# Two heads' attention scores in one step, their matmuls alternating between the two halves of TensorE's rows

## The chip, the cores and the metric

The kernel runs on one core of one Trainium2 chip. The metric is the device time of one execution in microseconds (us). Five engines work side by side: TensorE (PE in the profile, its weight loads PEld), VectorE (DVE), ScalarE (ACT), GpSimd (POOL) and SyncE (SP, which issues the weight DMAs). Each executes its own instructions in the order in which the program issues them and waits on semaphores of the others.

## The reference

Two transformer blocks run one after the other on 256 tokens of width 1024, in float32. The first has an even layer (differential attention and a convolution) and an odd one (a state space model and a latent attention), each with a gated feed-forward part. The second block has two layers. Each has two attentions over the same normalized input, both with 8 query heads of dimension 64:

```python
# kind "n": 256 own tokens with a bias, and 256 context tokens
s_win = einsum(qg, kg) * SCALE + bias;  s_ctx = einsum(qg, k_ctx) * SCALE
p = softmax(concatenate([s_win, s_ctx], -1));  o = p_win @ vg + p_ctx @ v_ctx
# kind "g": grouped, 2 key heads for 8 query heads, keys of x and of the context
s = einsum('bgrqd,bgkd->bgrqk', q, k_all) * SCALE;  o = softmax(s) @ v_all
```

Their results are merged with gates, projected, and followed by a gated feed-forward part. In the first of the two layers the 256 context tokens go through the same two attentions, but over the context alone.

## The kernel before

Activations are kept transposed (features on the 128 partitions, tokens along the free axis). Every dense product is made in three matmuls of split operands (`mm3`, L369 to L371; `token_steps`, L827 to L829): a weight is split into a high and a low part by ScalarE (`uh`, L349) and VectorE (`ul`, L350), a unit of 8 x 128 weights at a time.

The work is cut into steps held in queues, and `ORDER`, a string written out by hand, says in which order the queues give their steps: `m` is the main chain, `c` the chain of the context, `d` the modulation, `a` the attentions of the second block over x and the context, `x` the gates' projections, `k` small masks. So in the attentions of the second block, runs of `a` steps stand between single `x` or `m` steps. The program is issued in that order, and no engine reorders it for us.

`attention2` (L1844) makes the attentions of the second block. An item is a kind, one of two query tiles of 128 (`qt`) and a head. With two key sources (512 keys, n = 1) an item is one head; for the context alone (256 keys, n = 2) it is the heads h0 and h0 + 2, side by side in one PSUM bank. `pipeline` gives each item three steps: `scores`, then in the next round `trans`, then `out` one round later. Within one round the order is scores(i), out(i - 2), trans(i - 1).

- `scores` takes a PSUM bank of the tag "s" and makes per key source one float32 matmul with 64 rows: head h lies on the partitions 64 (h % 2) to 64 (h % 2) + 63. The profile shows each as two weight loads and two passes (L1861). Then it calls `softmax`.
- `softmax` (L852) puts off its work: `peak` (for kind "n" over x first the bias, L1867; maximum, L875; negation, L879) runs on VectorE, then `exp` (L869) on ScalarE. Each is issued when the steps issued meanwhile have used up a planned cost, 0.6 and then 1.0.
- `trans` forces its own item's `peak` and `exp` out if they aren't issued, takes another "s" bank, transposes the four blocks of 128 probabilities on TensorE (L893), and ScalarE copies them to SBUF (`probT`, L895). VectorE makes the reciprocal of the sums (L886).
- `out` does nothing for an even head. For an odd one it makes the products with the values of that head and the one before (L1891, 16 passes) and the reciprocals' broadcast (L1894, 4 passes) in the one bank "n"; ScalarE (L1908) and VectorE (L1903) take them out.

There are three "s" banks, taken in turn. `ps` (L203) counts the softmaxes whose `exp` is not issued and issues the oldest before a tag would run out:

```python
while tag == "s" and sum(k for _, k in self.held) + n > 3:
    self.undefer(self.held[0][0])
```

The even layer of the first block (L1041 to L1053) makes its scores in another form: two matmuls on the two halves of the rows into two banks, in one step.

Of the kernel before, what the change touches and what calls it, by code (L numbers as in the profile page):

```python
# [13 lines left out]
ALU = mybir.AluOpType  # L14
# [3 lines left out]
P = 128  # L18
T = 256
# [133 lines left out]
class Kern:  # L153
# [1690 lines left out]
    def attention2(self, st, kvs, local, kinds="ng"):  # L1844


        nc = self.nc
        d = {}
        K = T * len(kvs)
        n = 512 // K  # L1850

        def scores(it):
            kind, qt, h0 = it
            ps = self.ps("s").rearrange("p (g k) -> p g k", g=n)
            for a in range(n):
                h = h0 + 2 * a
                b = slice(64 * (h % 2), 64 * (h % 2) + 64)
                q = st[kind + "q"][b, h // 2, P * qt:P * qt + P]
                for i, kv in enumerate(kvs):
                    k = kv["nk"][b, h // 2, :] if kind == "n" else kv["gk"][b, (h // 4 + h) % 2, :]  # L1860
                    nc.tensor.matmul(ps[:, a, T * i:T * i + T], lhsT=q, rhs=k, start=True, stop=True)  # L1861
            pre = None
            if kind == "n" and local:
                def pre():
                    w = st["bias"][:, 6 * h0 + 2 - 2 * qt:6 * h0 + 6 - 2 * qt, ::-1]
                    v = ps[:, 0, :T].rearrange("p (j u) -> p j u", u=64)
                    nc.vector.tensor_tensor(v, v, w, ALU.add)  # L1867
            self.softmax(ps, n, 1.0 if kind == "n" else 0.125, K, d, it, pre)

        def trans(it):  # L1870
            self.undefer((id(d), it))
            pt, sm = d[it]
            t, r = self.transpose_prob(pt.rearrange("p g k -> p (g k)"), 512), self.recip(sm)
            for a in range(n):
                d[it[0], it[1], it[2] + 2 * a] = t[:, K * a:K * a + K], r[:, a:a + 1]

        def out(it):

            kind, qt, h0 = it
            if h0 % 2 == 0:  # L1880
                return
            o = self.ps("n").rearrange("p (a g t) -> p a g t", a=2, t=P)
            nk = K // P
            for g in range(n):
                m = h0 // 2 + g
                two = [d.pop((kind, qt, 2 * m + a)) for a in range(2)]
                for i in range(nk):
                    kv, k = kvs[i // 2], i % 2
                    for a in range(2):
                        c = 64 * (2 * m + a if kind == "n" else m // 2)  # L1890
                        nc.tensor.matmul(o[64 * a:64 * a + 64, 0, g, :], lhsT=kv[kind + "v"][:, k, c:c + 64],  # L1891
                                         rhs=two[a][0][:, P * i:P * i + P], start=i == 0, stop=i == nk - 1)
                for a in range(2):
                    nc.tensor.matmul(o[64 * a:64 * a + 64, 1, g, :], lhsT=two[a][1].to_broadcast([P, 64]), rhs=self.ident,  # L1894
                                     start=True, stop=True)
            m = h0 // 2
            if m == 0:
                d[kind, qt] = self.w2("oh", [P, 4, P])
            oh = d[kind, qt]
            R = self.w1("sr")[:, :P * n].rearrange("p (g t) -> p g t", g=n)  # L1900

            def norm():
                nc.vector.tensor_tensor(oh[:, m:m + n, :], o[:, 0, :n, :], R, ALU.mult)  # L1903
                if m + n == 4:
                    self.defer(0, lambda: st["ysink"](kind, qt, d.pop((kind, qt))))

            def factor():
                nc.scalar.activation(R, o[:, 1, :n, :], AF.Copy)  # L1908
                self.defer(0, norm)

            self.defer(0, factor, key="n")

        heads = (0, 1, 4, 5) if n == 2 else range(8)
        items = [(kind, qt, h) for kind in kinds for qt in range(2) for h in heads]
        return self.pipeline(items, [(scores, 0.86, 0), (out, 0.5 * n, 2), (trans, 0.44, 1)])

    def gate_steps(self, st, l, pool=None):

# [139 lines left out]
    def second_block(self, X, C):  # L2058

        steps = []  # L2060
        rope = lambda: (X["rC"], X["rS"])
        self.queues.update(a=[], x=[], k=[])
        keys = [dict(n="c", pn="ck", pg="ck", spill=C["spill"]) for _ in range(2)]

        def tables(l):
            if l == 0:
                self.open("ck", "right")
                self.new_kv(keys[0], ("gk", "gv", "nk", "nv"))
                for k in ("gk", "gv", "nk", "nv"):
                    self.unspill(keys[0], k, keys[0][k])  # L2070
            else:
                self.open("y2")
            self.open("pg", "left" if l else "right")
            self.open("ph", "left" if l else "right")
            X.update(pn="ph", pg="pg")
            X["rC"], X["rS"] = self.table("pg", "xc"), self.table("pg", "xs")

        def room(l):
            if l == 0:
                self.close("ar")  # L2080
                self.open("y2")
            self.open("gs", "right" if l else "left")
            self.ysplit(X, "y2")

        def end_att():
            self.close("ph")
            self.open("ph")

        def end_merge(l):
            for k in ("ph", "pg", "gs", "ck", "y2"):  # L2090
                self.close(k)
            self.open("ph")

        for l in range(2):
            load, mask = self.na_bias(X, l)
            steps.append(Step(lambda l=l: tables(l), after=[] if l else [self.spilled]))
            steps += self.modulated(X, l, 0)
            p1, p2 = self.proj_steps(X, l, rope)
            steps += [load] + p1
            steps.append(Step(lambda l=l: room(l), after=self.queues["c"][-1:]))  # L2100
            free = steps[-1]
            steps += p2
            mask[0].after.append(load)
            gates = self.gate_steps(X, l, "gs")
            gates[0].after.append(free)
            att = self.attention2(X, [X, keys[l]], True, "gn") + [Step(self.undefer)]
            att[0].after.append(p1[-1])
            for x in att[:-1]:
                fn, (kind, qt, h) = x.what
                if (fn, kind, qt) == ("scores", "n", 0):  # L2110
                    x.after += [p2[-1], mask[h]] + (last[-1:] if l else [])
                if l and x is att[0]:
                    x.after.append(self.last_a)
                if (fn, kind, qt, h) == ("out", "g", 0, 7):
                    x.after.append(free)
            self.queues["a"] += att
            self.queues["x"] += gates
            self.queues["k"] += mask
            steps.append(Step(end_att, after=[att[-1], gates[-1]]))
            steps += self.merge_steps(X, l) + self.wo_steps(X, l)  # L2120
            steps.append(Step(lambda l=l: end_merge(l)))
            if l == 0:
                last = self.last_keys(C, keys[1])
                last[0].after.append(steps[-1])
                self.queues["c"] += last
            steps += self.modulated(X, l, 1) + self.ffn2(X, l)
            steps.append(Step(lambda: self.close("ph")))
        return steps
# [143 lines left out]
```

## Time and profile before

| | |
|---|---|
| median of 3 runs | 2039.46 us (2037.99 to 2041.78) |
| the profiled execution | 2035.8 us, its span 2034.0 us |
| busy: PE, PEld, DVE, ACT, POOL | 95%, 88%, 67%, 49%, 4% of the span |
| mean granted TensorE clock | 0.978 |
| chain that ended last, by engine | PE 76%, DVE 14%, ACT 4%, DMA 4%, issue 2% |
| the same by line, L1861 | 4% |

The span runs from the first to the last instruction; the execution's own time is 1.8 us longer, and the median of the runs lies 3.7 us above that. A line such as `L893 PE MATMUL pss<-consts,prob` names the source line, the engine, the operation and the tiles written and read (`psd`, `pss`, `psn` are PSUM banks of the tags d, s, n). An end in brackets such as `[0.36 <-ACT prob L869]` is the time for which the engine was idle before it, and what ended that. The recorded time of a matmul contains its passage through the array, so matmuls that follow each other overlap in the records; what a group costs is read from its start to the start of what follows.

### The profile page before, as it was taken

The page shows a single profiled execution, that of the slowest core. Times are in us where ns is not written, and L with a number is a line of the kernel's source. Part 1 is how long each engine was busy: PE and PEld are TensorE (multiplying, and loading weights), DVE is VectorE, ACT ScalarE, POOL GpSimd, SP SyncE. Part 2 cuts the span into 40 slices and gives each one's busy share as a digit, 9 for nine tenths or more (in the row PEclk, how much of TensorE's full clock was granted, in tenths as well). Part 3 has the DMA queues.
Part 4 walks back from the last instruction along what each step waited for, and adds up shares of the span by engine and source line. Part 5 has one row for each costly group of instructions (what it writes and reads, how often), then busy time and mean ns, then how long its engine had stood idle before and what let it go on. Part 6 is the DMA issues. An engine that isn't in the chain of part 4 may idle for free.

```text
span 2034.0 us, 38003 instructions
## 1 busy us (share of the span) xinstructions
PE 1927.8 (95%) x15646; PEld 1785.2 (88%) x15646; DVE 1361.2 (67%) x2655; ACT 988.7 (49%) x1680; POOL 71.9 (4%) x112
## 2 busy tenths in 40 slices
PE   8889999999989999989996999989999899979998
PEld 7678889999878999789996888889999888879998
DVE  6997668777778678666655745676655755566554
ACT  5355665444445453554443455445444455535443
POOL 0212000000000000000001100000000100000000
PEclk9999999999989999999998999999999999999999
DMA  7756636666748665766556633345555643244553
GB/s 255 247 193 207 195 110 201 202 218 220 230 133 241 205 187 141 236 200 217 194 174 188 156 101 86 122 145 173 182 175 199 159 120 89 81 149 158 179 177 109
DMA packets 383775, 353.51 MB, mean 174 GB/s; under 512 B 14705, under 2 KB 370545, under 8 KB 383089
## 3 DMA queue, kind: packets, MB, share of 16 engines
q1 hardware_dynamic: 378336, 333.77, 51.9%
q0 software_dynamic: 4688, 15.73, 3.3%
q8 instruction: 123, 2.02, 0.4%
q10 hardware_dynamic: 576, 1.57, 0.2%
q14 instruction: 52, 0.42, 0.1%
HBM read 344.36 MB, written 6.68 MB: 173 GB/s over the span
## 4 chain that ended last, share of the span: by engine, by line
PE 76%; DVE 14%; ACT 4%; DMA 4%; issue 2%; SPq 0%; ACTq 0%; DVEq 0%
PE psd L369 21%; PE psd L371 20%; PE psd L370 20%; DVE ul L350 4%; PE pss L1861 4%; ACT uh L349 3%; PE pss L893 2%; PE psn L1891 2%; DMA raw<-in_w_in 2%; DVE cy L999 1%; PE psd L1657 1%; DMA raw<-in_l_w_in 1%; DMA raw<-in_w_mod 1%; PE psd L827 1%; DVE xres L592 1%
## 5 line engine op out<-in xcount | busy, mean ns | idle before, releaser
L350 DVE TENSOR_TENSOR ul<-raw,uh 128x1024 fp32r<-128x1024 f32 (+3 forms) x556 | 657.5, 1190 | 365.3 <-ACT uh L349 363.3
L349 ACT ACTIVATE uh<-raw 128x1024 fp32r<-128x1024 f32 (+3 forms) x556 | 566.0, 1025 | 337.1 <-PE psd L370 272.3
L369 PE MATMUL psd<-xacth,uh 128*128 128x256 f32 x2192 | 633.9, 289 | 9.9 <-ACT grp L703 3.1
L371 PE MATMUL psd<-xacth,ul 128*128 128x256 f32 x2192 | 626.2, 286 | 5.1 <-DVE ul L350 5.1
L370 PE MATMUL psd<-xactl,uh 128*128 128x256 f32 x2192 | 626.2, 286 | 0.6 <-DVE xactl L599 0.5
L369 PEld LDWEIGHTS psd<-xacth,uh 128*128 128x128 f32 x2192 | 425.8, 194 | 28.2 <-issue 13.4
L371 PEld LDWEIGHTS psd<-xacth,ul 128*128 128x128 f32 x2192 | 425.9, 194 | 6.6 <-DVE ul L350 6.5
L370 PEld LDWEIGHTS psd<-xactl,uh 128*128 128x128 f32 x2192 | 426.0, 194 | 1.9 <-DVE xactl L599 1.0
L369 PE MATMUL psd<-slot,uh 128*128 128x256 f32 x896 | 256.0, 286 | 0.5 <-ACT uh L349 0.5
L371 PE MATMUL psd<-slot,ul 128*128 128x256 f32 x896 | 251.4, 281 | 2.6 <-DVE ul L350 2.6
L370 PE MATMUL psd<-slot,uh 128*128 128x256 f32 x896 | 251.0, 280 | 0.0
L371 PE MATMUL psd<-hh,ul 128*128 128x256 f32 x704 | 198.1, 281 | 0.6 <-DVE ul L350 0.3
L369 PE MATMUL psd<-hh,uh 128*128 128x256 f32 x704 | 198.0, 281 | 0.0
L370 PE MATMUL psd<-hl,uh 128*128 128x256 f32 x704 | 197.5, 280 | 0.0
L369 PEld LDWEIGHTS psd<-slot,uh 128*128 128x128 f32 x896 | 169.6, 189 | 7.4 <-issue 5.2
L371 PEld LDWEIGHTS psd<-slot,ul 128*128 128x128 f32 x896 | 169.3, 189 | 3.3 <-DVE ul L350 3.3
L370 PEld LDWEIGHTS psd<-slot,uh 128*128 128x128 f32 x896 | 169.4, 189 | 0.0
L371 PEld LDWEIGHTS psd<-hh,ul 128*128 128x128 f32 x704 | 132.0, 188 | 1.6 <-DVE ul L350 1.6
L369 PEld LDWEIGHTS psd<-hh,uh 128*128 128x128 f32 x704 | 132.5, 188 | 0.4 <-issue 0.4
L370 PEld LDWEIGHTS psd<-hl,uh 128*128 128x128 f32 x704 | 132.5, 188 | 0.0
L869 ACT ACTIVATE prob<-pss,nm 128x512 f32<-128x512 f32 (+2 forms) x124 | 70.2, 568 | 22.3 <-DVE nm L879 18.9
L875 DVE TENSOR_REDUCE mx<-pss 128x1 f32<-128x512 f32 (+1 forms) x80 | 55.2, 689 | 34.4 <-PE pss L1861 33.2
(480 smaller groups left out, 2528.4 us busy)
## 6 DMA issues: line engine op xcount, KB each, us to landing
raw<-in_w_mod SPq DMA_DIRECT2D x48, 1024.0 KB, 5.5
raw<-in_w_ffn_in SPq DMA_DIRECT2D x40, 1024.0 KB, 5.1
raw<-in_w_in SPq DMA_DIRECT2D x32, 1024.0 KB, 5.7
raw<-in_w_ffn_in SPq DMA_DIRECT2D x52, 512.0 KB, 5.2
raw<-in_w_in SPq DMA_DIRECT2D x48, 512.0 KB, 5.2
raw<-in_w_ffn_out SPq DMA_DIRECT2D x24, 1024.0 KB, 4.9
raw<-in_l_w_gate SPq DMA_DIRECT2D x20, 1024.0 KB, 5.3
raw<-in_l_w_up SPq DMA_DIRECT2D x20, 1024.0 KB, 5.3
```

Of the source, the lines that this page charges most:

```text
L349: self.nc.scalar.activation(q.h, src, AF.Copy)
L350: self.nc.vector.tensor_tensor(q.l, src, q.h.bitcast(F32), ALU.subtract)
L369: mm(ps, lhsT=wh, rhs=ah, start=start, stop=False)
L370: mm(ps, lhsT=wh, rhs=al, start=False, stop=False)
L371: mm(ps, lhsT=wl, rhs=ah, start=False, stop=stop)
L592: nc.vector.tensor_tensor(x(m), x(m), d.pop(m), ALU.add)
L827: mm(d[i][j], lhsT=ah[:, s], rhs=u.h[:, k, :], start=kk == 0, stop=False)
L869: nc.scalar.activation(pt[:, g, :], ps[:, g, :] if one else ps[g], AF.Exp, bias=nm[:, g:g + 1], scale=scale, accum_out=sm[:, g:g + 1])
L875: nc.vector.tensor_reduce(mx, ps, AX.X, ALU.max)
L893: self.nc.tensor.transpose(t[:, k * P:(k + 1) * P], w[:, k * P:(k + 1) * P], self.ident)
L1861: nc.tensor.matmul(ps[:, a, T * i:T * i + T], lhsT=q, rhs=k, start=True, stop=True)
L1891: nc.tensor.matmul(o[64 * a:64 * a + 64, 0, g, :], lhsT=kv[kind + "v"][:, k, c:c + 64], rhs=two[a][0][:, P * i:P * i + P], start=i == 0, s ...
```

## The change

The even item's `scores` step now makes the scores of its own head(s) and of the next odd ones. It takes two banks, and the matmuls alternate between the rows 0 to 63 (even head, first bank) and 64 to 127 (odd head, second bank). Both softmaxes are put off from there, the even one first. The odd item's `scores` step does nothing. The planned cost of the step in the pipeline is 0.65 for 0.86, and the masks that the first pair of kind "n" needs are required for both heads. `ORDER` is as it was, and so are `trans` and `out`.

```diff
         def scores(it):
             kind, qt, h0 = it
-            ps = self.ps("s").rearrange("p (g k) -> p g k", g=n)
+            if h0 % 2:
+                return
+            two = [self.ps("s", 2 - j).rearrange("p (g k) -> p g k", g=n) for j in range(2)]
             for a in range(n):
-                h = h0 + 2 * a
-                b = slice(64 * (h % 2), 64 * (h % 2) + 64)
-                q = st[kind + "q"][b, h // 2, P * qt:P * qt + P]
                 for i, kv in enumerate(kvs):
-                    k = kv["nk"][b, h // 2, :] if kind == "n" else kv["gk"][b, (h // 4 + h) % 2, :]
-                    nc.tensor.matmul(ps[:, a, T * i:T * i + T], lhsT=q, rhs=k, start=True, stop=True)
-            pre = None
-            if kind == "n" and local:
-                def pre():
-                    w = st["bias"][:, 6 * h0 + 2 - 2 * qt:6 * h0 + 6 - 2 * qt, ::-1]
-                    v = ps[:, 0, :T].rearrange("p (j u) -> p j u", u=64)
-                    nc.vector.tensor_tensor(v, v, w, ALU.add)
-            self.softmax(ps, n, 1.0 if kind == "n" else 0.125, K, d, it, pre)
+                    for j in range(2):
+                        h = h0 + 2 * a + j
+                        b = slice(64 * j, 64 * j + 64)
+                        q = st[kind + "q"][b, h // 2, P * qt:P * qt + P]
+                        k = kv["nk"][b, h // 2, :] if kind == "n" else kv["gk"][b, (h // 4 + h) % 2, :]
+                        nc.tensor.matmul(two[j][:, a, T * i:T * i + T], lhsT=q, rhs=k, start=True, stop=True)
+            for j, ps in enumerate(two):
+                pre = None
+                if kind == "n" and local:
+                    def pre(ps=ps, h=h0 + j):
+                        w = st["bias"][:, 6 * h + 2 - 2 * qt:6 * h + 6 - 2 * qt, ::-1]
+                        v = ps[:, 0, :T].rearrange("p (j u) -> p j u", u=64)
+                        nc.vector.tensor_tensor(v, v, w, ALU.add)
+                self.softmax(ps, n, 1.0 if kind == "n" else 0.125, K, d, (kind, qt, h0 + j), pre)
...
-        return self.pipeline(items, [(scores, 0.86, 0), (out, 0.5 * n, 2), (trans, 0.44, 1)])
+        return self.pipeline(items, [(scores, 0.65, 0), (out, 0.5 * n, 2), (trans, 0.44, 1)])
...
-                    x.after += [p2[-1], mask[h]] + (last[-1:] if l else [])
+                    x.after += [p2[-1], mask[h], mask[h | 1]] + (last[-1:] if l else [])
```

## Rows read from the trace of the kernel before

**Rows 1.** Busy time of each engine, context attentions, a slow stretch, both layers' attentions.

```profile
core 0: us, PE busy (x) PEld busy (x) DVE busy (x) ACT busy (x) POOL busy (x), PEclk, DMA share, GB/s
178.00:316.00 138.00, 132.34 (x1080) 117.85 (x1077) 98.44 (x251) 87.08 (x208) 9.40 (x16) 0.99 0.56 173
285.80:289.90 4.10, 4.10 (x29) 3.21 (x28) 3.10 (x8) 1.91 (x6) 0.00 (x0) 0.58 0.70 227
1161.00:1300.00 139.00, 138.33 (x1066) 114.36 (x1064) 72.37 (x157) 76.14 (x150) 0.07 (x1) 1.00 0.32 92
1628.00:1767.00 139.00, 138.11 (x1076) 114.31 (x1075) 70.51 (x155) 76.56 (x151) 0.00 (x0) 1.00 0.32 92
```

**Rows 2.** Chain of waits within 1161 to 1300 us: shares by line.

```profile
by line: PE pss L1861 23.6%; PE psd L369 14.4%; PE psd L370 12.6%; PE psd L371 12.6%; PE pss L893 12.3%; PE psn L1891 11.8%; PE psd L827 3.1%; PE psd L828 2.7%; PE psd L829 2.6%; PE psn L1894 2.5%; ACT probT L895 0.8%; ACT prob L869 0.6%; i
```

**Rows 3.** Timeline of TensorE at 1628 us (start, duration, what): two heads, nothing between.

```profile
1628.45 0.71 PE L1861 MATMUL pss<-xgk,xgq 64*128 64x256 f32 x4
1628.99 0.60 PE L1861 MATMUL pss<-cgk,xgq 64*128 64x256 f32 x4
1629.52 0.50 PE L827 MATMUL psd<-uh,xacth 128*128 128x512 f32 x1
```

**Rows 4.** Timeline of TensorE at 1213 us: transposes, one head's scores, products, transposes.

```profile
1212.82 0.66 PE L893 MATMUL pss<-consts,prob 128*128 128x128 f32 x4
1213.40 0.70 PE L1861 MATMUL pss<-xgk,xgq 64*128 64x256 f32 x2
...
1214.46 0.66 PE L1891 MATMUL psn<-probT,xgv 128*64 128x128 f32 x8
...
1215.71 0.66 PE L893 MATMUL pss<-consts,prob 128*128 128x128 f32 x4
```

**Rows 5.** Timeline of TensorE at 1264 us: transposes with a gate's matmuls behind them.

```profile
1263.69 0.66 PE L893 MATMUL pss<-consts,prob 128*128 128x128 f32 x4
1264.10 0.36 PE L369 MATMUL psd<-xacth,uh 128*128 128x256 f32 x1
```

**Rows 6.** Timeline of ScalarE at 1214 us: the copy of the transposes of rows 4.

```profile
1213.57 0.60 ACT L895 ACTIVATE probT<-pss 128x512 f32<-128x512 f32 x1 [0.59 <-PE pss L893]
```

**Rows 7.** Timeline at the end of the first layer's attentions: transposes, products directly behind.

```profile
1296.89 1.09 PE L893 MATMUL pss<-consts,prob 128*128 128x128 f32 x8
...
1298.72 0.30 PEld L1891 LDWEIGHTS psn<-probT,xnv 128*64 128x64 f32 x5 [0.31 <-ACT probT L895]
...
1299.96 0.39 PE L369 MATMUL psd<-xacth,uh 128*128 128x256 f32 x1
```

**Rows 8.** Groups within 1161 to 1300 us: count, busy us, mean ns, idle before.

```profile
L350 DVE TENSOR_TENSOR ul<-raw,uh 128x1024 fp32r<-128x1024 f32 x24 | 29.4, 1224 | 13.3 <-ACT uh L349 13.3
...
L349 ACT ACTIVATE uh<-raw 128x1024 fp32r<-128x1024 f32 x23 | 24.2, 1056 | 4.3 <-PE psd L370 1.7 <-ACT prob L869 1.4 <-PE psd L829 1.2
L875 DVE TENSOR_REDUCE mx<-pss 128x1 f32<-128x512 f32 x32 | 22.1, 691 | 18.4 <-PE pss L1861 17.8
L869 ACT ACTIVATE prob<-pss,nm 128x512 f32<-128x512 f32 x32 | 21.9, 684 | 2.5 <-DVE nm L879 1.9 <-DVE ri L886 0.3
...
L895 ACT ACTIVATE probT<-pss 128x512 f32<-128x512 f32 x32 | 19.0, 597 | 18.0 <-PE pss L893 18.0
...
L1867 DVE TENSOR_TENSOR pss<-pss,bias 128x256 f32<-128x256 f32 x16 | 6.9, 432 | 16.3 <-PE pss L1861 16.3
...
L879 DVE TENSOR_SCALAR nm<-mx 128x1 f32<-128x1 f32 x32 | 4.9, 154 | 1.1
```

**Rows 9.** Timeline of TensorE at 1283 us: transposes that wait for their exponentials.

```profile
1283.49 0.66 PE L893 MATMUL pss<-consts,prob 128*128 128x128 f32 x4 [0.36 <-ACT prob L869]
```

**Rows 10.** Chain of waits within 178 to 316 us: start, duration, what.

```profile
198.19 1.07 PE pss L1861 x4
...
285.88 1.49 PE pss L1861 x4
...
311.39 1.06 PE pss L1861 x4
```

## The prediction

> **What bounds the kernel now.** I read the page first: TensorE is busy for 95% of the span and makes 76% of the chain that ended last. The attentions fill three stretches, so I read the busy time there [rows 1]: TensorE 138 of 139 us in both layers over x, against 72 and 71 for VectorE and 76 and 77 for ScalarE; 132 of 138 us where the context's attentions run among other chains. The reader is to see that in the two later stretches nothing but TensorE can set the time, at the full granted clock (2.4 GHz). The chain inside the first of them puts 23.6% on L1861, the line of the change, more than on any other [rows 2]; that is 33 us of 139 for 32 scores steps. Then I read the timeline of TensorE block by block, since the change moves blocks and leaves their order.
>
> **What two heads cost together.** One head's scores take 1.06 us from their start to the start of what follows (1213.40 to 1214.46) [rows 4]. The trace of before holds one place where two heads stand directly behind each other, at the head of the second layer: eight passes start at 1628.45 and the next matmul at 1629.52, so 1.07 us for two heads [rows 3]. The four passes over own keys are listed before the four over the context's, although the program issues all of one head first: the two halves run beside each other. So a pair costs 1.07 us, and each odd step taken out leaves the time of a whole block, less 0.01.
>
> By the Trainium skill (TensorE: Matmul & The Clock Gate, Part 3, "The mechanism") matmuls start and end strictly in program order and only weight loads overtake. Rows 3 show the second head's first passes ahead of the first head's last ones, so the trace differs from that rule here, and I go by the trace; what strict order would make of the time is a rival below.
>
> **What is taken out.** Over x there are 32 odd steps, 16 a layer; one is paired already (rows 3), so 31 go. What each is worth hangs on what stands behind it. Walking through both stretches I count 16 with a gate's or a value projection's matmuls behind them (for one of them transposes), and 15 that stand between the transposes of one odd head and `out`, which needs these very transposes.
>
> The 16: transposes to scores 0.58, scores 1.06 [rows 4]; transposes straight to a gate's matmuls 0.41 [rows 5], since no change between 64 and 128 rows is left. 0.58 + 1.06 - 0.41 = 1.23 each, 19.7 us.
>
> The 15: here the odd scores are the cover for ScalarE's copy. Transposes to `out` take 1.64 us now (1212.82 to 1214.46) [rows 4]. The copy of them starts 0.75 us after they start and takes 0.60 [rows 6], so the odd head's half of `out` can start after 1.35 plus some 0.05. The stretch's end shows the case without a scores step between [rows 7]: the second of two sets of transposes starts at about 1296.89 + 0.41 = 1297.30, the products that need its copy at 1298.72, 1.42 us later, after a wait for `probT`; from there to the next block is 1.24 us, a whole `out`. So 1.64 - 1.40 = 0.24 us is left of each, 3.6 us. Bounds: if the even head's products cover the copy, the full 1.06 (12.3 us more in all); if one weight split, 1.06 us [rows 8], always stands before the copy on ScalarE, 0.82 lost on each (15.9 us less). I take the value of rows 7: ScalarE was idle for 18.0 us before the 32 copies of a stretch, waiting for the transposes in all of it [rows 8], so it was nearly always free when they came.
>
> **What moves.** The odd head's softmax is issued one round earlier, behind the even one's. VectorE then makes two in a row: 0.43 bias, 0.69 maximum, 0.15 negation [rows 8], 1.36 with the gaps for kind "n", 0.9 without bias. The even head's transposes lie later than its exponentials in every case that I worked out. The three banks taken in turn are the new wait: two rounds take four banks, so the next pair's even scores land in the bank of this pair's odd scores and wait for its exponential. Behind them on TensorE everything queues. With no filler between, the next pair comes 1.07 + 1.40 + 1.24 + 0.58 = 4.29 us after this one; the pair's last pass ends at 1.14 (1628.99 + 0.60 - 1628.45) [rows 3], so the second "n" softmax ends at 1.14 + 2 x 1.36 + 0.68 + 0.05 = 4.59, so a wait of 0.3 to 0.45; the kind without bias ends at 3.7 and waits for nothing. Five places of kind "n" have no filler: 2 us lost. Bounds: nothing, and with a low split (1.22) before them on VectorE at the nine fillerless places of both kinds, 15. A wait that goes: the transposes at 1283.49 wait 0.36 us for an exponential that will now be long made [rows 9], and so once in the other layer: 0.7 us. No DMA is added or moved; the shares of 0.32 leave room.
>
> Over x: 19.7 + 3.6 + 0.7 - 0.3 - 2.0 = 21.7 us.
>
> **The context's stretch.** Eight odd steps go. The chain there runs through six of them; rows 10 show the first, the slow one (285.88) and the last. Two, at 182 and 294 us, are not in it: VectorE's convolution and a normalization end later there, and they bring nothing. Five at 1.06 and one at 1.49 make 6.8; row changes would add up to 1, and VectorE, 71% busy here [rows 1], may take some back. All `out` steps here have fillers before them. I take 6.3, with 0 and 9 as ends.
>
> **Sum.** 21.7 + 6.3 = 28.0 us of the profiled execution's 2035.8, so 2007.8; the runs' median lies 3.7 us higher: 2011.5 us.
>
> **The rivals.**
> - *The copy is covered* (0.08). `out` begins with the even head's products while the odd copy runs, and the waits stay away: 12.3 + 2 us more, 1997. For it: ScalarE is 55% busy. Against: rows 7, where it waited.
> - *Strict order* (0.04). A matmul's second pass must start before the other half's first, so of every two passes only one is hidden: five pass times in place of four. A pass is (1.06 - 0.17) / 4 = 0.22 us, the 0.17 being the row change (0.58 less 0.41) [rows 4, 5]; for 39 pairs 8.6 us: 2020. Rows 3 speak against it. (This is the rule of the Trainium skill named above.)
> - *Softmax takes over in the fillerless runs* (0.12). There a pair leaves TensorE some 3.5 us of work, while ScalarE needs 2 x (0.68 + 0.60) and readouts, VectorE 2 x 1.36 and reciprocals, so any extra op sets the time: 15 places at 1 us, 2026. For it: the balance in those runs; against: whole stretches have 76 us of ScalarE in what will be 128. (The Trainium skill, TensorEngine Tiling, "PSUM Bottleneck", warns that packing speeds the array and not the emptying of PSUM; by rows 1 that binds in these runs at most.)
> - *Late bank, slower* (0.05). If the odd exponential is late at every pair, with a low split in front of it on VectorE (0.4 + 1.22), all 31 pairs wait 1.6 us: 50 us lost, 2059. It decides from 0.9 us a pair (28 / 31). Against: most pairs have a filler of about 3 us between.
> - *The halves don't overlap when alternated* (0.03). Two heads then cost 2.1 us as before, only row changes go, and the 15 waits of 0.82 and the banks stay: some 11 us slower, 2050. Rows 3 speak against it.
> - *Given back later* (0.06). What follows waits for weights that can't come earlier: 2036 to 2040. For it: the DMA is 56% busy in the context's stretch; against: 32% in the other two.
>
> A fall of the granted clock belongs to the waits: 285.8 to 289.9 ran at a mean of 0.58, mostly the lower level (1.2 GHz), after an idle TensorE, and the scores there took 1.49 [rows 1, 10]. My waits are below 1 us each, and around rows 9 nothing slowed.
>
> **How the numbers follow.** Forecast 0.62, its own range 2005 to 2020. Of the 0.38 left, 0.24 is faster too. The range 2000 to 2028 takes in the softmax case, the strict order and most of the covered one. A change under 0.2% (4 us) can't be told here from none. Faster 0.87, same 0.05, slower 0.08.
>
> **What would show it.** L1861: pairs of 1.07 us at 40 places, TensorE's busy time about 30 us less. A new wait of `out` for `probT` of 0.3 to 0.8 us at 15 places, and of L1861 for `prob` at about five. Both stretches over x 11 us shorter, the context's 6. Wrong would be: pairs of 1.3 or 2.1 us, waits over 1 us at most pairs, or shorter attentions with a longer rest.

## The result: 2018.97 us, and the profile after

The median fell from 2039.17 us (4 runs) to 2018.97 us (4 runs, 2015.73 to 2025.85), a ratio of 0.9904 [0.9876, 0.9931], about 20 us; forecast were 2011.5 us and 28 us. The profiled execution after took 2025.85 us (span 2023.1), 6.9 above the median of its runs, so the two traces are compared by stretches and not by their spans.

The lines behind the change moved: the scores' matmuls are L1865 now, the bias L1872, the products L1896, the reciprocals' broadcast L1899, ScalarE's copy of it L1913, VectorE's product with that copy L1908. First the busy time of each engine in the three stretches of attentions, after (start:end, length, busy time and instructions of each engine, granted clock, DMA share, GB/s), to be held against [rows 1]. A stretch over x is cut here and below from the first scores matmul to the first matmul behind the last `out`.

```profile
core 0: us, PE busy (x) PEld busy (x) DVE busy (x) ACT busy (x) POOL busy (x), PEclk, DMA share, GB/s
178.90:317.00 138.10, 128.64 (x1102) 117.60 (x1098) 98.52 (x255) 87.36 (x208) 9.41 (x16) 0.98 0.57 173
1166.60:1296.10 129.50, 124.16 (x1058) 104.55 (x1057) 69.82 (x157) 76.14 (x149) 0.05 (x1) 1.00 0.34 99
1629.70:1756.20 126.50, 122.33 (x1069) 104.55 (x1068) 68.75 (x154) 75.70 (x149) 0.00 (x0) 1.00 0.35 101
```

Cut the same way, the stretches of before are 138.0 us (to 1299.96 [rows 7]) and 137.9 us (from 1628.45 [rows 3]). So 8.5 us went in the first layer and 11.4 us in the second. That alone is 19.9 us, all of what the medians lost. The context's stretch, cut between the same two instructions (177.14 to 316.02 us before, 177.88 to 314.31 after), is 2.5 us shorter in this trace; over all runs it gave next to nothing, as shown further down. New beside [rows 1] is that TensorE no longer fills its stretches: 5.3 and 4.2 us are idle, where 0.7 and 0.9 were.

The chain of waits within 1166 to 1296 us, shares by line, answers to [rows 2]: scores fell from 23.6% to 13.3%, while VectorE's maximum (L875) and bias (L1872), which were not listed there, now carry 9.4%.

```profile
by line: PE psd L369 13.5%; PE pss L1865 13.3%; PE psd L370 12.7%; PE psd L371 12.7%; PE pss L893 10.1%; PE psn L1896 8.9%; DVE mx L875 6.4%; PE psn L1899 3.4%; PE psd L827 3.3%; DVE pss L1872 3.0%; PE psd L828 2.8%; PE psd L829 2.8%; ACT p
```

Where the idle time comes from stands in two timelines of one place without filler. TensorE (start, duration, engine, line, operation, tiles, count, and in brackets the idle time before it and what ended it):

```profile
1256.79 0.70 PE L1865 MATMUL pss<-xnk,xnq 64*128 64x256 f32 x4
1257.32 0.60 PE L1865 MATMUL pss<-cnk,xnq 64*128 64x256 f32 x4
1257.85 0.66 PE L893 MATMUL pss<-consts,prob 128*128 128x128 f32 x4
1258.44 0.43 PE L1896 MATMUL psn<-probT,xnv 128*64 128x128 f32 x2
1259.26 0.54 PE L1896 MATMUL psn<-probT,xnv 128*64 128x128 f32 x5 [0.39 <-ACT probT L895]
...
1260.68 0.43 PE L1899 MATMUL psn<-consts,ri 128*64 128x128 f32 x2 [0.33 <-DVE ri L886]
1261.04 0.66 PE L893 MATMUL pss<-consts,prob 128*128 128x128 f32 x4
```

Eight passes cost 1.06 us (1256.79 to 1257.85), the forecast price. The products start with the even head's two passes and then wait for the odd head's copy: 1.41 us after the transposes began, the 1.40 of the forecast. But `out` doesn't end there. Its broadcast stops a second time, for the reciprocals, and the block takes 2.60 us (1258.44 to 1261.04) where it took 1.25 [rows 4]. VectorE at the same place shows why:

```profile
1257.95 0.43 DVE L1872 TENSOR_TENSOR pss<-pss,bias 128x256 f32<-128x256 f32 x1 [1.01 <-PE pss L1865]
1258.42 0.69 DVE L875 TENSOR_REDUCE mx<-pss 128x1 f32<-128x512 f32 x1
1259.14 0.15 DVE L879 TENSOR_SCALAR nm<-mx 128x1 f32<-128x1 f32 x1
1259.22 0.42 DVE L1872 TENSOR_TENSOR pss<-pss,bias 128x256 f32<-128x256 f32 x1
1259.67 0.69 DVE L875 TENSOR_REDUCE mx<-pss 128x1 f32<-128x512 f32 x1
1260.40 0.15 DVE L879 TENSOR_SCALAR nm<-mx 128x1 f32<-128x1 f32 x1
1260.47 0.21 DVE L886 RECIPROCAL ri<-sm 128x1 f32<-128x1 f32 x2
```

The sum that this `out` waits for belongs to the pair before and was made before the transposes at 1257.85 could start. But `trans` issues its reciprocal (L886) behind the new pair's two biases and maxima, and VectorE keeps that order: 2.5 us of work (1257.95 to 1260.47), where one head's 1.3 stood before.

The waits of TensorE's weight loads (waiting line, what ended the wait, total us, times, longest), first those of the first layer's stretch, then of the second's:

```profile
PEld psn L1896 <- ACT probT L895: 6.6, 11, 0.9
PEld psn L1899 <- DVE ri L886: 2.6, 5, 0.6
...
PEld psn L1896 <- ACT probT L895: 4.5, 8, 0.6
PEld psn L1899 <- DVE ri L886: 1.8, 2, 1.2
```

Now the context's stretch. Its pairs want two of the three "s" banks at once. The first pair's weight loads, after:

```profile
178.88 0.29 PEld L1865 LDWEIGHTS pss<-slot 64*128 64x128 f32 x2 [0.41 <-ACT slot L1791]
180.89 0.73 PEld L1865 LDWEIGHTS pss<-slot 64*128 64x128 f32 x6 [1.71 <-ACT prob L869]
```

The odd head's bank is held by another chain's softmax; TensorE's weight loads stand still for 1.71 us (its matmuls for 1.31) in the middle of the pair. The fifth pair waits in its middle too, for a bank that another chain's VectorE step still reads:

```profile
251.70 0.73 PEld L1865 LDWEIGHTS pss<-slot,slot 64*128 64x128 f32 x6 [0.90 <-DVE xactl L391]
```

At the other end, VectorE of after at 293 us, and the second of its maxima as it stood before:

```profile
293.20 0.68 DVE L875 TENSOR_REDUCE mx<-pss 128x2 f32<-128x512 f32 x1
...
294.00 0.68 DVE L875 TENSOR_REDUCE mx<-pss 128x2 f32<-128x512 f32 x1
...
299.66 0.68 DVE L875 TENSOR_REDUCE mx<-pss 128x2 f32<-128x512 f32 x1
```

At 299.66 us, before, it stands behind the normalization (L589 to L599) that the chain runs through here; now it stands in the middle of it. TensorE's wait there, then the busy time in slices of 2 us (columns as above), three of after and two of before:

```profile
291.65 0.80 PE L893 MATMUL pss<-consts,prob 128*128 128x128 f32 x4 [1.77 <-ACT probT L895]
...
290.00:292.00 2.00, 0.34 (x3) 0.35 (x4) 2.00 (x7) 1.20 (x3) 0.00 (x0) 1.00 0.00 0
292.00:294.00 2.00, 2.00 (x12) 2.00 (x11) 1.97 (x7) 0.81 (x2) 0.00 (x0) 0.51 0.04 8
294.00:296.00 2.00, 2.00 (x13) 2.00 (x13) 1.97 (x7) 0.36 (x1) 0.05 (x1) 0.64 0.00 0
...
292.00:294.00 2.00, 0.41 (x4) 0.17 (x3) 2.00 (x8) 1.19 (x4) 0.00 (x0) 1.00 0.00 0
294.00:296.00 2.00, 2.00 (x13) 1.61 (x14) 2.00 (x5) 1.00 (x2) 0.00 (x0) 1.00 0.04 8
```

After, TensorE was idle for most of 290 to 292 us, since the transposes there waited 1.77 us for a copy (`probT`), and then ran mostly at the lower level (1.2 GHz) until about 295. Before, the slices from 290 to 302 are all granted 1.00. An earlier fall (285.8 to 289.9 us before [rows 1], 284 to 290 after) stands in both traces and costs the same 1.7 us, counted as length times the missing share of the clock.

### The profile page after: what moved, and what is told of

Read it like the earlier page. It is cut to its first block, busy times and chain, and to the rows that moved or that the text cites. A ratio compares the mean times of both kernels' runs of the same rounds, so it can differ in the third digit from the quotient of the medians.

```text
span 2023.1 us, 37981 instructions
## 1 busy us (share of the span) xinstructions
PE 1899.8 (94%) x15646; PEld 1765.9 (87%) x15646; DVE 1358.2 (67%) x2655; ACT 989.3 (49%) x1680; POOL 72.6 (4%) x112
## 4 chain that ended last, share of the span: by engine, by line
PE 55%; DVE 9%; ACT 4%; DMA 2%; issue 2%; ACTq 0%; SPq 0%; DVEq 0%
PE psd L369 15%; PE psd L371 15%; PE psd L370 15%; DVE ul L350 3%; ACT uh L349 2%; PE pss L1865 2%; DMA raw<-in_w_in 2%; PE pss L893 1%; PE psn L1896 1%; PE psd L1657 1%; DVE mx L875 1%; PE psd L827 1%; PE psd L828 1%; PE psd L829 0%; DVE pr L1979 0%
## 5 line engine op out<-in xcount | busy, mean ns | idle before, releaser
L456 DVE TENSOR_TENSOR acc<-acc,sq 128x256 f32<-128x256 f32 x116 | 49.1, 423 | 43.2 <-ACT sq L455 41.6
```

Source lines behind the costliest of these rows:

```text
L456: self.nc.vector.tensor_tensor(acc, acc, s, ALU.add)
```

## The experiments

The theory: two heads cost the time of one because the two halves of the rows work side by side; the rest follows from what stood beside the removed steps (copy, softmax, banks). Each run is timed against before on its own chip. An edit moves the lines below it, so an operation can stand under another number in a run; its tiles name it (`pss<-xnk,xnq` are scores, `pss<-consts,prob` transposes, `psn<-probT` products).

**All of the even head first, then all of the odd head.** If the gain lay in the alternation, it would go.

```diff
-            for a in range(n):
-                for i, kv in enumerate(kvs):
-                    for j in range(2):
+            for j, a in [(j, a) for j in range(2) for a in range(n)]:
+                for i, kv in enumerate(kvs):
```

> All of the even head's matmuls are issued before the odd head's, in the same step. Theory (the two halves of the rows run side by side whatever the program order): pairs stay at 1.07 us, the time stays with the changed kernel's 2019 us. Rival (matmuls keep program order, only the alternation brings the overlap): pairs of 2.1 us, 40 of them, some 40 us more, 2060 us.

2014.2 us, ratio 0.9881 [0.9849, 0.9912]; stretches 129.3 and 126.6 us, as after. TensorE:

```profile
1259.99 0.71 PE L1865 MATMUL pss<-xnk,xnq 64*128 64x256 f32 x4
1260.53 0.60 PE L1865 MATMUL pss<-cnk,xnq 64*128 64x256 f32 x4
1261.07 0.66 PE L893 MATMUL pss<-consts,prob 128*128 128x128 f32 x4
```

1.08 us for the pair. The order within a pair is worth nothing; what counts is that both heads stand together.

**The same, with one 128-row matmul of a single column between the two heads.** It needs both halves, so the heads can't overlap. Everything else (two banks, one step, softmax earlier) stays.

```diff
+                if j and not a:
+                    nc.tensor.matmul(two[1][:, 0, 0:1], lhsT=self.ident, rhs=self.ident[:, 0:1], start=True, stop=True)
```

> As e1, but a one-column matmul over all 128 rows stands between the two heads, so that they can't overlap; the place of the steps and of the softmaxes is the changed kernel's. Theory (the whole gain is the overlap): a pair costs 2.2 us or more, 1.15 to 1.4 us more at 40 places, some 50 us more than the changed kernel, about 2065 us, slower than before by 25. Rival (the gain is that softmaxes are issued earlier): it stays below 2030 us.

2066.46 us, 1.0122 [1.0094, 1.0151]; stretches 148.6 and 146.3 us, some 19.5 us longer than after in each.

```profile
1228.98 0.70 PE L1867 MATMUL pss<-xgk,xgq 64*128 64x256 f32 x2
1229.52 0.59 PE L1867 MATMUL pss<-cgk,xgq 64*128 64x256 f32 x2
1230.04 0.38 PE L1860 MATMUL pss<-consts 128*128 128x1 f32 x2
1230.35 0.70 PE L1867 MATMUL pss<-xgk,xgq 64*128 64x256 f32 x2
1230.89 0.59 PE L1867 MATMUL pss<-cgk,xgq 64*128 64x256 f32 x2
1231.41 0.66 PE L893 MATMUL pss<-consts,prob 128*128 128x128 f32 x4
```

2.43 us for the pair in place of 1.06. Of these the added matmul takes 0.31 itself (1230.04 to 1230.35), so two heads that can't overlap cost 2.12, twice one. Without the 0.31 at 40 places, 12 us, the time would be some 2054 us, still above before's 2043.97 on that chip: without the overlap the new waits make the change a loss, and the overlap alone pays for them.

**`out` one round later.** This puts another pair between an odd head's transposes and its products.

```diff
-        return self.pipeline(items, [(scores, 0.65, 0), (out, 0.5 * n, 2), (trans, 0.44, 1)])
+        return self.pipeline(items, [(scores, 0.65, 0), (out, 0.5 * n, 3), (trans, 0.44, 1)])
```

> `out` one round later (3 for 2), the rest as changed: the next pair's scores and an even head's transposes now lie between an odd head's transposes and its `out`. Theory (15 places lose 0.8 us to the copy and some 9 of them 0.5 us more to the reciprocal behind two maxima): both waits go, each layer's attentions 6 to 9 us shorter, 2004 us. Rival (in these runs the softmax chain on VectorE and ScalarE sets the time): the wait moves to L893 for `prob`, the time stays near 2019 us.

2021.77 us, 0.9908 [0.9884, 0.9931]. Over x it gains (124.9 and 124.6 us, 6.5 in all), but two sets of transposes now stand directly behind each other, and the second waits for its exponential (6.4 us at four places of the first layer); and the context's stretch, whose `out`s come later too, loses about 9 us. A mixed run: it shows that the copy wait can be covered and that the softmax is next.

**The reciprocals issued right behind the exponentials.** If the second wait is VectorE's order, it goes.

```diff
+            if early:
+                d[it] = pt, self.recip(sm)
...
-            t, r = self.transpose_prob(pt.rearrange("p g k -> p (g k)"), 512), self.recip(sm)
+            t = self.transpose_prob(pt.rearrange("p g k -> p (g k)"), 512)
```

> The reciprocal of the sums is issued right behind its exponential and not in `trans`, where it stands behind the next pair's two maxima on VectorE. Theory: the waits of L1899 for `ri` (4 us in the first layer, 3.1 in the second) go, `out` falls from 2.60 to 2.05 us at seven places, 4 to 6 us in all: 2014 us. Rival (VectorE waits for the exponential at the head of its queue, and the low splits or the bias behind it come late): 2019 us or more.

2021.06 us, 0.9904 [0.9879, 0.9928]; stretches 128.1 and 125.5 us. The wait of the broadcast is gone, and but for one (2.33 us) no `out` takes more than 2.05 us, so the cause of that wait is shown. But only 2.4 of its 4.4 us came out of the stretches, and the median shows no gain over the changed kernel. What took the place is the late bank of the forecast, at five places of kind "n", three in the first layer and two in the second. One of them, on TensorE and in its weight loads:

```profile
1271.05 0.94 PE L1867 MATMUL pss<-xnk,xnq 64*128 64x256 f32 x3
...
1272.56 0.39 PE L369 MATMUL psd<-xacth,uh 128*128 128x256 f32 x1
...
1271.51 0.18 PEld L1867 LDWEIGHTS pss<-xnk,xnq 64*128 64x128 f32 x1 [0.17 <-ACT prob L869]
```

1.51 us for a pair that costs 1.06, since the bank it wants is still read by the last pair's exponential; the other four take 1.40 to 1.52. Together that is 1.9 us.

**The fillers spread.** The gates' and value projections' steps that `ORDER` places among the attentions over x keep their sequence, but stand one at a time (two or three early on) directly before the odd `out`s, so that each copy has a cover.

```diff
-        self.run(self.merge(self.chains(), self.ORDER))
+        self.run(self.merge(self.chains(), respread(self.ORDER, plans)))
```

`respread` rewrites the order between the first and the last `a` step of each layer: in the first, two stand before the first `trans`, then 2, 2, 3, 2 and one each before the odd `out`s; in the second two, then five times 2 and one each (the last odd `out` has none).

> The changed kernel with another order: in both layers' attentions the gate and projection steps between the attention steps stand one (early two) directly before each odd head's `out`, where 15 of them had none; their own sequence is kept. Theory (what the change gives back over x is the wait of `out` for the copy, 0.8 us at 15 places, and for the reciprocal): both waits go, each stretch falls from 129.5 and 126.5 us to 119 to 122, 2006 us. Rival (softmax on VectorE and ScalarE has become the bound of these runs): the waits move to L893 and L1865, the stretches stay above 125 us, 2017 us or more.

2002.02 us, 0.9796 [0.977, 0.9822]: 118.3 and 119.2 us, 38.4 less than before in both stretches together. Its busy time:

```profile
1172.00:1290.30 118.30, 118.30 (x1058) 102.72 (x1057) 69.39 (x157) 75.51 (x148) 0.05 (x1) 1.00 0.38 107
1614.90:1734.10 119.20, 118.80 (x1070) 103.47 (x1069) 68.36 (x154) 76.20 (x149) 0.00 (x0) 1.00 0.38 107
```

TensorE is full again. One place of it (transposes, a filler from 1255.47, `out`, transposes):

```profile
1255.06 0.66 PE L910 MATMUL pss<-consts,prob 128*128 128x128 f32 x4
...
1258.51 0.66 PE L1913 MATMUL psn<-probT,xnv 128*64 128x128 f32 x8
1259.00 0.61 PE L1913 MATMUL psn<-probT,cnv 128*64 128x128 f32 x8
1259.43 0.39 PE L1916 MATMUL psn<-consts,ri 128*64 128x128 f32 x4
1259.75 0.66 PE L910 MATMUL pss<-consts,prob 128*128 128x128 f32 x4
```

`out` takes 1.24 us, without a wait in it.

**That order in the kernel before.**

```diff
-        self.run(self.merge(self.chains(), self.ORDER))
+        self.run(self.merge(self.chains(), respread(self.ORDER, plans)))
```

> The order of e5 in the kernel before, whose heads are made one by one. Theory: TensorE waited for nothing there, so the order alone brings nothing: stretches of 137 to 139 us, 2039 us. Rival (the order is a gain of its own): below 2033 us.

2038.76 us, 0.9994 [0.9977, 1.001]; 137.0 and 138.0 us. Before, the odd scores were the cover, and another order brings nothing. Only with the pairs is it worth about 17 us by the medians (18.5 in the two stretches).

**Pairs over x alone, and pairs for the context alone** (the other kind keeps the old `scores`).

```diff
+        if n == 2:
+            return self.pipeline(items, [(single, 0.86, 0), (out, 0.5 * n, 2), (trans, 0.44, 1)])
```

and the same with `n == 1`.

> Pairs only in the attentions over x; the context's heads are made one by one as before. Theory (in the context's stretch the pairs wait for their second bank, which other chains hold, and the six steps' time is given back there): the time of the changed kernel within 3 us, 2019 us, the stretch from 178 to 316 us no longer than its own by more than 2.5. Rival (the context's pairs bring the 6 us forecast): 2025 us.

> Pairs only in the context's attentions; over x one head at a time as before. Theory: 0 to 3 us less than before, 2037 us, both stretches over x at 138 us. Rival (they bring 6 us): 2033 us.

2024.82 us, 0.9912 [0.9887, 0.9937], and 2038.15 us, 0.999 [0.9968, 1.0012]. The intervals of the first and of the whole change overlap widely, and the second holds 1: over x lies the gain, and the context's pairs bring nothing that can be measured. (The 6.3 us forecast for them would be a ratio of 0.9969, just inside that interval; the profiles, below, are the stronger evidence.)

**ScalarE's copy over x made twice**, to see whether `out` waits for it.

```diff
-        self.defer(0, lambda: self.nc.scalar.activation(o[:, :keys], t[:, :keys], AF.Copy))
+        def copy():
+            for _ in range(1 + again):
+                self.nc.scalar.activation(o[:, :keys], t[:, :keys], AF.Copy)
+        self.defer(0, copy)
```

> The changed kernel with ScalarE's copy of the transposes over x made twice over (the same values, 0.6 us more each, 64 times). Theory (`out` waits for that copy wherever no filler covers it): 0.6 us more at the 9 to 15 places, less where the reciprocal comes still later; the first layer's stretch 132 to 135 us for 129.5, the second's 128.5 to 131 for 126.5, 2024 to 2028 us in all. Rival (the copy is covered, something else makes the waits): both stretches within 1 us of the changed kernel's.

2030.2 us, 0.9948 [0.9927, 0.9969]; 135.6 and 132.9 us, 6.1 and 6.4 more, somewhat above the range of the theory. The wait doubles at the same 11 places of the first layer, from 6.6 us:

```profile
PEld psn L1900 <- ACT probT L897: 12.8, 11, 1.2
```

So it is the copy that `out` waits for. In the first layer the 2.6 us of waits for the reciprocals are gone in return, hidden behind the longer copy, and the transposes wait 4.6 us in place of 2.3 for a bank that a copy still reads.

**The copy twice with the fillers spread.**

```diff
-        self.run(self.merge(self.chains(), self.ORDER))
+        self.run(self.merge(self.chains(), respread(self.ORDER, plans)))
...
+            for _ in range(1 + again):
```

> The same doubled copy in the order of e5, where a filler stands before each `out`. Theory: the fillers of 2.9 us cover 1.2 us of copies: stretches within 1.5 us of e5's 118.3 and 119.2, 2003 us. Rival (ScalarE's load of 19 us more a layer sets the time): 125 us or more each.

2011.81 us, 0.9856 [0.982, 0.9893]; 123.2 and 125.2 us, 4.9 and 6.0 more than with the fillers spread alone, so the theory's 1.5 us failed. `out` waits no longer at the places with a filler, as the covered copy lets expect; but the time came back at the transposes, which want the bank that the copy empties (here, and then with single copies):

```profile
PEld pss L910 <- ACT probT L914: 9.9, 15, 0.7
...
PEld pss L910 <- ACT probT L912: 5.0, 15, 0.3
```

I had not expected that wait. Even where the copy is covered for `out`, it holds one of three banks.

**The fillers spread, pairs over x alone.**

```diff
+        if n == 2:
+            return self.pipeline(items, [(single, 0.86, 0), (out, 0.5 * n, 2), (trans, 0.44, 1)])
```

> The order of e5 with pairs only over x; the context's heads are made one by one as before. Theory (the context's pairs bring nothing): e5's 2002 us within 3. Rival (they bring 6 us): 2008 us.

2001.46 us, 0.9815 [0.9775, 0.9854], the same stretches (118.3 and 119.2 us). Together with the fillers spread under both kinds of pairs, this is the best of all kernels run, some 38 us under before; the two can't be told apart.

## Why the prediction was right, and which step failed

**Two heads in 1.06 us: right.** 1.06 or 1.07 at all 32 pairs over x and at five of the context's eight (the other three stand in a wait), where [rows 3] gave 1.07 from a single one. The split run shows that it is the overlap. *The halves don't overlap when alternated* and *Strict order* (a pair at 1.28) fall. By the Trainium skill (TensorE: Matmul & The Clock Gate, Part 3, "The mechanism") matmuls start in program order; with all of the even head issued first the trace still has a pair in 1.08 us with the odd head's own-key passes listed ahead of the even head's context passes, so here the measurement decides, and heads in separate runs of matmuls overlap as alternated ones do.

**The 16 places with other work behind, 19.7 us, and the uncovered copy, 12.3 us given back at the 15: right.** I count 15 `out`s without filler after, nine and six, which take 16.5 us more than 1.24 each. 4.4 of that are the waits for the reciprocals; what is left, 12.1, is the copy's. The run with the copy twice shows the cause. The 16 places are measured only as what is left. The 15 give 15 x 1.06 - 16.5 = -0.6 us, the two waits that went give 0.9, the pairs' 0.01 us takes 0.3. These cancel, so the measured 19.9 us are theirs, against 19.7. *The copy is covered* falls for the change itself. The spread fillers cover the copy by another way than that rival's (the even head's products), and the order with a filler before each odd `out` comes near its 1997 us (2002.02).

**The late bank, 2.0 us: the term had another cause, and was too small.** I let the second "n" softmax be late for the next pair's bank. The pair does not come that early: the broadcast of `out` waits first, 4.4 us in seven waits, behind the same VectorE work. My step read what VectorE's queue does for the softmax and not what else is issued behind it there: the reciprocals of `trans`. The sum put that second wait at nothing, and this is its step that failed over x. With the reciprocals moved ahead the late bank appears at five places, 0.34 to 0.46 us each and 1.9 in all, where the forecast had five places, 0.3 to 0.45 us and 2.0. *Softmax takes over* holds in direction only: 4.4 us over the 15 places, where it had 1 us at each.

Over x the sum was 21.7 us and 19.9 were measured; the 2.4 us between 4.4 and 2.0 are more than the whole gap. The rest of the miss, from 28 us to about 20, is the context's.

**The context, 6.3 us: this step failed.** I took "five at 1.06 and one at 1.49", the pieces of the chain that lie on L1861 [rows 10], as time that goes when the steps go. The pairs alone in the context are worth 0.999 [0.9968, 1.0012]. In the stretch from 177 to 316 us, cut between the same two instructions, the profiles of the seven kernels with these pairs and unmoved `out`s are 2.5, 1.9, 1.0 and 0 us shorter and three times 0.5 us longer than before; in the three others whose context heads are made one by one it differs by at most 0.1.

TensorE's time in these profiles says where the gain went. The eight odd steps are 8.5 us of work at 1.06 each. With the pairs TensorE is idle for 3.8 to 6.1 us more than before, and the lower clock takes more: length times the missing share of the clock, over slices of 2 us, is 1.7 us in all four profiles without these pairs, 3.4 in four with them and 6.8 in the three that are 0.5 us longer. One such slice, of the run with pairs for the context alone, behind a wait of TensorE of 2.12 us for ScalarE's split of a weight (`uh`), with ScalarE busy all the time:

```profile
304.00:306.00 2.00, 2.00 (x11) 2.00 (x11) 1.90 (x4) 1.50 (x3) 0.00 (x0) 0.50 0.09 16
```

Idle time, clock and the change in length together make 7.7 to 9.1 us in each of the seven. So the work did leave TensorE, and idle time and a second fall of the clock took its place. Of the idle time the trace after shows two mechanisms. First, the pair takes two of three banks at once among chains that hold banks too: the scores' loads wait 1.71 us in the middle of the first pair and 0.90 in the middle of the fifth. Second, the end of the stretch runs through VectorE's normalization; the second head's maximum and negation, 0.68 + 0.17 us, now stand in it. How much each of these adds to the time alone, and why the clock's falls last longer in three of the runs, no run shows. The Trainium skill (TensorEngine Tiling (Array Packing), Gotcha 1, "PSUM Pressure") says that row tiles write to different banks; the 1.71 us above are what a second bank costs where other chains hold the banks. *Given back later* had what follows wait for weights that can't come earlier. Between the two layers' stretches nothing is given back: the ten profiles with the heads over x paired have 329.2 us there in the mean, the three without 328.7. The context's part was lost inside its own stretch; from its end to the first scores over x the profiles take 846 to 852 us without its pairs and 850 to 856 with them, so that a part was given back there too is not excluded. *Late bank, slower* falls.

**The rest.** The profiled span after is only 10.9 us shorter. Between the stretches (314 to 1167 us, and 1296 to 1630) it is 6.4 and 5.1 us longer. The change doesn't touch these parts, and they vary by that much without it: the first x attention begins at 1161.9 us before, at 1168.2 with the order spread in before, which issues the same instructions up to there, and at 1165.4 and 1164.8 in the two runs without context pairs. The clock varies as well: from 560 to 760 us the lower level takes 6.8 us before and 11.5 with the order spread in before, counted as above. A profile of before that began late would have looked better for the change; the medians and the stretches are what counts.

## What to carry to other kernels

A step that is taken out of a full engine's stream gives back its time only where something else stands behind it; where it covered another engine's work, price that engine's latency, and place a filler there in the same change (20 us became 38 so). When two softmaxes are issued in a row, walk through everything that the in-order engine gets behind them, small operations for earlier items too. A piece of the chain in a stretch where several engines and chains share banks is an upper bound of a gain and not its size.

## What the hardware showed that I had not expected

Matmuls on opposite halves of the rows overlap even where all passes of one head are issued ahead of all of the other (1.08 us): in the order of steps no engine reorders the program, but TensorE interleaves these passes. And a single 128-row matmul of one column between them costs 1.35 us (2.43 against 1.08): 0.31 for itself and 1.04, the whole overlap. Behind an idle time of 1.77 us the clock fell to 1.2 GHz at 292 us after, and before it did not behind a similar one in the slice of 292 to 294 us (TensorE busy 0.41 of 2 us, then 1.00). Identical instructions took up to 6 us more or less over the first 1160 in four executions, not all on one chip, and the granted clock varied with them; so a profile's span alone can't settle a change of 10 us here.
